# Pool maps and scales multiplied once into the pool projection's weight, and the background work's rates set anew

## The chip, the cores and the metric

The kernel runs on one core of one Trainium2 chip. The metric is the device time of one execution in microseconds, as the median of several runs. TensorE multiplies, VectorE (DVE) and ScalarE (ACT) work element by element, and SyncE (SP) and a few other queues issue transfers between device memory and on-chip memory.

## The reference

One residual block over 2048 tokens of width 1024, all in fp32:

```python
h = rmsnorm(x, norm_mix_pre)
proj = h @ w_in                                   # pool 512 | GLU 1024 | gate_a 1024 | gate_b 1024
pooled = trailing_mean_minus_self(u_pool, ...)    # 4 groups of 128 channels, windows 2, 4, 8, 16
mixed = einsum('bsgc,gcd->bsgd', pooled, pool_w) * pool_scale
branch_a = mixed @ w_pool_out
branch_b = silu(layernorm(causal_depthwise_conv(a * sigmoid(g), 31 taps))) @ w_conv_out
merged = sigmoid(g_a) * branch_a + sigmoid(g_b) * branch_b
x = x + rmsnorm(merged @ w_o)
f = square(relu(rmsnorm(x) @ w_up)) @ w_down
x = x + rmsnorm(f)
```

The part that matters here is branch A: a 128x128 matrix `pool_w[g]` for each group, a scale for each channel, and then the projection `w_pool_out` (512 by 1024). All three are linear, and nothing stands between them.

## The kernel before

The 2048 tokens are worked on as two batches (`b`) of 1024, each with two halves (`t`) of 512. Every fp32 operand of a product is split into a high part and a low part of a shorter format: ScalarE casts the high part (`split`, `split_w`, line L202 or L209), VectorE subtracts it to get the low part (`sub`, L123). Each product of blocks is then three passes of 128x512 matmuls (high by high, low by high, high by low; `matmuls`, L252).

The large projections save products as Strassen's method does: an `Octet` covers a group of blocks with 7 products instead of 8. Its weights are sums and differences of raw weight blocks (`weight_parts`: raw loads `wr`, sums `ws`, high and low parts `wh` and `wl`), its tokens sums and differences of token blocks (`token_parts`: `big`, `tr`). `START` and `ORDER` list the order of the 7 products; `run_octets` goes through them. In batch 0, the first GLU octet is followed by the second (`o2`) interleaved with the pool octet (`pi`, from about 69 to 142 us), and then by the octets of gate a (`ga`) and gate b (`gb`), until about 307 us. Then come branch A of batch 0 (`branch_a`: mixed tokens times `w_po`), the same projections of batch 1 with the second half of the work of batch 0 in the background, both merges with the output projection, and the two large MLP products `up` and `down`, the longest part.

What isn't a product of an octet runs in the background. A generator yields after each small step, and a `Lane(rate, generators)` takes `rate` steps of its generators at every product (`bg()`); `yield n` skips n products. Such work is the convolution's taps (`conv_steps`, one VectorE operation a tap, L918, accumulating in `y`), the pool steps, the statistics of batch 1 (`in_stats`) and the norm of the convolution (`norm_steps`, which reloads the taps' sums `yd` and lets TensorE sum over channels, `rb`). A background instruction is tied to come behind the product at which it was taken. Nearly every load, and many stores, are issued by SP one after the other; some stores by ScalarE. A scheduler orders the instructions of each engine; `tc.high_priority(offset=n)` lets a block of code stand n instructions earlier in its priorities, as far as data allows.

The pool branch: `more()`, called at a given product of `pi`, runs `pool_weight()` (loads `w_pool`, splits it into `pw`) and adds `pool_steps(0)` to the lane `tail`. For each group `pool_steps` sums the window (VectorE), subtracts the token, splits the result (`split`), multiplies it with `pw` (6 matmuls into the accumulator `mix`), scales it while ScalarE copies it out, and stores it to `mxd`. `branch_a` reads it back and multiplies it with `w_po`. The lines that fix the pace:

```python
tail = Lane(1.3, conv_steps(0, (0,)))                  # 3 from more() on
lanes += [Lane(3.2, *rest, marked(norm_steps(0, 1), "norm"))]
lanes.append(Lane(1.7, marked(pool_steps(1, False), "pool")))
```

Of the kernel before, what the change touches and what calls it, by code (L numbers as in the profile page):

```python
# [15 lines left out]
P = 128  # L16
D = 1024
SEQ = 2048
T = 512
# [49 lines left out]
def block_kernel(  # L69
# [58 lines left out]
    def load(o, src):  # L128
        return nc.sync.dma_start(o, src)
# [150 lines left out]
    def weight_parts(src, key, b, keep, raw):  # L280


        s = {}

        def get(q):
            if q not in raw:
                raw[q] = mk(p_wr, "wr")
                load(raw[q], src[q])
            return raw[q]

        def minus(a, b, op=sub):
            o = mk(p_ws, "ws")
            op(o, a, b)
            return o

        def source(i):
            if i in (1, 2, 4):
                return get({1: 0, 2: 1, 4: 3}[i])
            if (key, i, "sum") in kept and b:
                if ("s", i) not in raw:  # L300
                    raw["s", i] = mk(p_wr, "wr")
                    load(raw["s", i], kept[key, i, "sum"])
                return raw["s", i]
            if i == 7:
                return minus(get(0), get(2))
            if i in (5, 6) and 1 not in s:
                s[1] = minus(get(2), get(3), add)
            if i == 6:
                s[2] = minus(s[1], get(0))
                return s[2]  # L310
            if i == 5:
                return s[1]
            return minus(get(1), s[2])

        def save(i, what, tile):
            kept[key, i, what] = dram("kept")
            later.append((kept[key, i, what], f32(tile)))

        def part(i):
            with tc.high_priority(offset=ahead[0]):  # L320
                for q in {1: (0,), 2: (1,), 4: (3,), 7: (0, 2), 5: (2, 3), 6: (2, 3, 0), 3: (1,)}[i]:
                    if (key, i, "sum") not in kept or not b:
                        get(q)
                if (key, i, "sum") in kept and b:
                    source(i)
            with tc.high_priority(offset=60):
                t = source(i)
                w = raw.pop(("w", i), None)
                if w is None and not ((key, i, "low") in kept and b):
                    w = split_w(t)  # L330
            if (key, i, "low") in kept and b:
                with tc.high_priority(offset=80):
                    w = split_w(t, low=kept[key, i, "low"])
            if keep and not b:
                save(i, "low", w[1])
                if keep == "sums" and i not in (1, 2, 4):
                    save(i, "sum", t)
            return w

        return part  # L340
# [652 lines left out]

    pw = [p_const.tile([P, CW], F32R, tag=f"pw{i}", name=f"pw{i}") for i in (0, 1)]

    def pool_weight():
        raw = mk(p_wr, "wr")[:, :CW]
        load(raw, w_pool)
        nc.scalar.copy(pw[0], raw)
        sub(pw[1], raw, f32(pw[0]))  # L1000

    def pool_steps(b, alone):

        def get(g):
            s, u = window(W), tr()
            load(s, ud[g][:, b * TB : b * TB + W])
            load(u, ud[g][:, HALO + b * TB : HALO + b * TB + TB])
            return s, u

        s, u = get(0)  # L1010
        yield 1
        for g in range(CC):
            w, m = WINDOWS[g], 1
            while m < w:
                lo = HALO - (w - 2 * m)
                s2 = window(W) if alone or m in (2, 8) else mk(p_ss, "r", F32, (P, W))
                add(s2[:, lo:], s[:, lo:], s[:, lo - m : W - m])
                s, m = s2, 2 * m
                yield
            if b == 0:  # L1020
                mul(
                    s[:, HALO : HALO + w],
                    s[:, HALO : HALO + w],
                    cst[:, C_CNT + g * HALO : C_CNT + g * HALO + w],
                )
            nc.vector.scalar_tensor_tensor(
                u, s[:, HALO:], 1.0 / w, u, op0=ALU.mult, op1=ALU.subtract
            )
            hl = split(u, *TR)
            if g + 1 < CC:  # L1030
                s, u = get(g + 1)
            yield 3
            ps = psum("mix")
            for t in (0, 1):
                h = slice(t * T, (t + 1) * T)
                matmuls(ps[:, h], pw, g, [tuple(p[:, h] for p in hl)], main=False)
            o = tr()
            nc.scalar.activation(o, ps, AF.Copy, scale=col(C_PSC + g))
            yield
            load(mxd[b, g, 0], o)  # L1040
            yield

    def cell_of(d, homes):

# [31 lines left out]
    def branch_a(b, mixed, bg):  # L1076


        def gate_of(k):
            sg = tr()  # L1080
            load(sg, sad[(b, *k)])
            return sg

        keys = [(c, t) for c in range(CPS) for t in (0, 1)]
        for (c, t), sg in ahead_by_one(keys, gate_of, 2):
            if t == 0:
                w = load_w(w_po[c], ("po", c))
            ps = psum("A")
            for q in (0, 1):
                i = matmuls(ps[:, q * T : (q + 1) * T], w, CC * q, half(mixed, t))  # L1090
            mark(i)
            flush()
            with tc.high_priority(offset=URGENT):
                mark(mul(sg, ps, sg))
            load(mad[b, c, t], sg)
            bg()
# [374 lines left out]
    o2, = glu(0, parts, ahead_raw[:1])  # L1471
    tail = Lane(1.3, conv_steps(0, (0,)))
    stats = Lane(1, in_stats(1))

    def then(f, o, at=4):

# [9 lines left out]

    def more():
        ahead[0] = AHEAD
        pool_weight()
        tail.gens.append(chain_of(pool_steps(0, True), conv_steps(0, (1, 2, 3), False)))  # L1490
        tail.rate = 3

    pi = pool_in(0, parts, ahead_raw[1])[0]
    ahead[0] = 45
    lanes.append(tail)
    then(lambda: lanes.append(stats), o2, 4)
    run(
        [o2],
        [then(more, pi, 4)],
        gate(0, parts, 3, sad, "ga", "lows"),  # L1500
        gate(0, parts, 5, sbd, "gb", "sums"),
    )
    stats.empty()
    rest = tail.gens
    mixed = fetch(mxd, 0)
    parts = Parts(lambda ops: input_parts(1, ops))
# [11 lines left out]
        yield from gen  # L1518

    rest = [marked(chain_of(*rest), "conv")]  # L1520
    lanes += [Lane(3.2, *rest, marked(norm_steps(0, 1), "norm"))]

    def pooling():
        lanes[0].rate = 3.2
        lanes.append(Lane(1.7, marked(pool_steps(1, False), "pool")))
        lanes.append(Lane(2.0, behind_all(conv_steps(1, (0, 1, 2, 3)), "conv", "pool")))


# [7 lines left out]
    )  # L1536
    conv1 = lanes.pop()
    empty()
    conv1.rate = 0.5
    lanes.append(conv1)  # L1540
    merged = merge(0, bg)
    fetched = []
# [16 lines left out]

    parts.need(2)  # L1560
    branch_a(1, mixed, step)
    conv1.rate = 1.2
    conv1.gens.append(norm_steps(1, 3))
    lanes.append(conv1)
    def faster():
        conv1.rate = 2.8

    octs = mlp_up(0, parts)
    then(faster, octs[0])
    run(octs)  # L1570
    empty()
    early.close()
# [469 lines left out]
```

## Time and profile before

| | us |
|---|---|
| median of 3 runs | 2219.32 (2218.80 to 2219.84) |
| profiled execution, its own time | 2218.82 |
| span of that execution, first to last instruction | 2216.9 |
| TensorE busy | 2168.8 (98%) |
| VectorE busy | 1683.1 (76%) |
| ScalarE busy | 1047.7 (47%) |

The mean granted clock of TensorE is 0.991 of full speed. A profile row such as `PE glu L252 <- ACT wh L209: 3.8, 1, 3.8` says that TensorE's matmuls into `glu` of line 252 waited 3.8 us in total, in 1 event, the longest 3.8, for ScalarE's instruction that wrote `wh` in line 209. A timeline row has the start in us, the time to the end of a group of alike instructions, the engine, line and operation, `out<-in`, sizes, how many, and in brackets the idle time before it and what ended it. A matmul's own duration (about 390 ns) overlaps its neighbours'.

### The profile page before, as it was taken

The numbers are of one execution on the slowest core, as the hardware profiler recorded it, in microseconds if no ns is written. First come the engines' busy times: TensorE is split into PE (matmuls) and PEld (weight loads), VectorE is DVE, ScalarE is ACT, GpSimd is POOL, SyncE is SP. The second block draws the span as 40 slices with busy tenths as digits, with TensorE's granted clock in tenths as the row PEclk, the third lists the DMA queues.
The fourth block names the chain that finished last, engine by engine and source line by source line (L and its number), as shares of the span: only waits on it lengthen the run. The fifth ranks groups of instructions, "written<-read, shape, count | busy, mean of one in ns | idle before, by whom it ended". The sixth has DMA issues, their size and how long they took to land.

```text
span 2216.9 us, 25038 instructions
## 1 busy us (share of the span) xinstructions
PE 2168.8 (98%) x9580; PEld 1787.5 (81%) x9580; DVE 1683.1 (76%) x1637; ACT 1047.7 (47%) x1102; POOL 20.6 (1%) x39
## 2 busy tenths in 40 slices
PE   9999999999999999999999999999999999999996
PEld 7777888778788888888888878788878888888875
DVE  8988688996789899977757857876644656696767
ACT  5434453334443535455735766665444222224553
POOL 0000000000000000000000000000000000000001
PEclk9999999999999999999999999999999999999998
DMA  4678898777997788354786778885957545446798
GB/s 169 242 286 300 294 364 291 240 246 273 328 376 258 250 328 293 144 210 153 273 306 234 249 264 287 330 312 210 357 196 233 181 155 189 149 146 224 267 306 253
DMA packets 157863, 563.31 MB, mean 254 GB/s; under 512 B 18576, under 2 KB 18704, under 8 KB 157712
## 3 DMA queue, kind: packets, MB, share of 16 engines
q1 hardware_dynamic: 141040, 500.90, 63.7%
q10 hardware_dynamic: 12672, 46.14, 5.3%
q0 software_dynamic: 4032, 14.68, 2.5%
q8 instruction: 75, 1.23, 0.2%
q14 instruction: 44, 0.36, 0.1%
HBM read 374.39 MB, written 188.31 MB: 254 GB/s over the span
## 4 chain that ended last, share of the span: by engine, by line
PE 82%; DVE 7%; DMA 6%; ACT 2%; issue 2%; SPq 0%; DVEq 0%; ACTq 0%; POOL 0%; POOLq 0%
PE down L252 26%; PE up L252 24%; PE wo L252 7%; PE gb L252 6%; PE glu L252 5%; PE B L252 4%; PE ga L252 4%; PE A L252 3%; DMA wr<-w_in 1%; DVE y L918 1%; DMA fo<-x1d 1%; PE pool L252 1%; DVE wl L123 1%; DVE tr L120 1%; PE rb L458 1%
## 5 line engine op out<-in xcount | busy, mean ns | idle before, releaser
L252 PE MATMUL up<-big,wh 128*128 128x512 f32 x1792 | 482.3, 390 | 1.7 <-DVE big L123 1.5
L252 PEld LDWEIGHTS up<-big,wh 128*128 128x128 f32 x1792 | 337.1, 188 | 73.2 <-DVE big L123 2.7
L209 ACT CAST wh<-wr 128x1024 fp32r<-128x1024 f32 x169 | 177.6, 1051 | 301.9 <-PE up L252 72.9
L252 PE MATMUL down<-tr,wh 128*128 128x512 f32 x800 | 312.5, 391 | 0.0
L918 DVE SCALAR_TENSOR_TENSOR y<-v,cst,y 128x1024 f32<-128x1024 f32 x240 | 307.7, 1282 | 2.8
L252 PE MATMUL down<-fo,wh 128*128 128x512 f32 x784 | 302.6, 391 | 1.1 <-ACT fo L1703 1.1
L252 PE MATMUL up<-big,wl 128*128 128x512 f32 x896 | 276.6, 390 | 0.0
L252 PE MATMUL down<-fo,wl 128*128 128x512 f32 x768 | 238.4, 392 | 2.8 <-DMA wl<-lows 2.8
L209 ACT CAST wh<-ws 128x1024 fp32r<-128x1024 f32 x118 | 123.9, 1051 | 212.4 <-PE up L252 63.3
L120 DVE TENSOR_TENSOR big<-big,down 128x1024 f32<-128x1024 f32 x88 | 107.0, 1219 | 121.5 <-PE down L252 111.7
L252 PEld LDWEIGHTS up<-big,wl 128*128 128x128 f32 x896 | 168.3, 188 | 34.9
L1703 ACT CAST fo<-tr 128x1024 fp32r<-128x1024 f32 x86 | 86.9, 1052 | 206.6 <-PE down L252 133.8
L123 DVE TENSOR_TENSOR wl<-ws,wh 128x1024 fp32r<-128x1024 f32 x110 | 134.3, 1221 | 58.6 <-ACT wh L209 54.4
L252 PEld LDWEIGHTS down<-tr,wh 128*128 128x128 f32 x800 | 150.9, 189 | 31.3
L252 PEld LDWEIGHTS down<-fo,wh 128*128 128x128 f32 x784 | 147.6, 188 | 32.3 <-ACT fo L1703 1.6
L252 PEld LDWEIGHTS down<-fo,wl 128*128 128x128 f32 x768 | 145.2, 189 | 33.4 <-DMA wl<-lows 3.2
L123 DVE TENSOR_TENSOR wl<-wr,wh 128x1024 fp32r<-128x1024 f32 x99 | 120.8, 1220 | 20.3 <-ACT wh L209 19.3
L123 DVE TENSOR_TENSOR tr<-tr,fo 128x1024 fp32r<-128x1024 f32 x86 | 101.8, 1220 | 43.8 <-ACT fo L1703 43.8
L252 PE MATMUL wo<-big,wh 128*128 128x512 f32 x480 | 128.8, 390 | 0.0
L252 PE MATMUL ga<-big,wh 128*128 128x512 f32 x448 | 121.1, 392 | 2.7 <-ACT tr L408 1.8
L252 PE MATMUL glu<-big,wh 128*128 128x512 f32 x432 | 117.9, 394 | 6.0 <-ACT wh L209 3.8
L252 PE MATMUL gb<-big,wh 128*128 128x512 f32 x448 | 120.9, 392 | 0.0
(196 smaller groups left out, 3367.1 us busy)
## 6 DMA issues: line engine op xcount, KB each, us to landing
tr<-fd SPq DMA_DIRECT2D x110, 512.0 KB, 4.5
wl<-kept SPq DMA_DIRECT2D x81, 512.0 KB, 4.5
kept<-wl SPq DMA_DIRECT2D x74, 512.0 KB, 5.5
wr<-w_down SPq DMA_DIRECT2D x68, 512.0 KB, 4.7
wr<-w_up SPq DMA_DIRECT2D x64, 512.0 KB, 4.4
wr<-w_in SPq DMA_DIRECT2D x56, 512.0 KB, 5.2
fd<-tr ACTq DMA_DIRECT2D x54, 512.0 KB, 3.6
fd<-tr SPq DMA_DIRECT2D x48, 512.0 KB, 3.5
```

Of the source, the lines that this page charges most:

```text
L120: return nc.vector.tensor_tensor(o, a, b, op=ALU.add)
L123: return nc.vector.tensor_tensor(o, a, b, op=ALU.subtract)
L209: nc.scalar.copy(hi[:, :n], src[:, :n])
L252: i = nc.tensor.matmul(ps, w[wp][:, (at + k) * P : (at + k + 1) * P], rhs[k][xp], start=start and n == 0, stop=stop and n == len(order) - ...
L458: nc.tensor.matmul(st[:, at + g : at + g + 1], ss[:, g * P : (g + 1) * P], inv_n, start=start is None or (start and g == 0), stop=stop, sk ...
L918: nc.vector.scalar_tensor_tensor(acc, v[:, k : k + TB], wk, acc, op0=ALU.mult, op1=ALU.add)
L1703: nc.scalar.copy(hi, t)
```

## The change

Since the three maps are linear, `pool_w`, `pool_scale` and `w_pool_out` are multiplied together on the chip once. A new generator `pool_weights` runs in a lane of its own (`weights`, rate 2), beside the second GLU octet's end and the first gate: it loads `w_pool` (which the host now hands over transposed), scales its four 128x128 blocks by `pool_scale`, splits them into `pw`, loads each of the four 128-row blocks of `w_pool_out`, splits it, multiplies (6 `mix` matmuls a block), copies the result and stores it in four pieces of 128 KB into `w_pp`, from which `branch_a` loads its weights in both batches. `pool_steps` stores the window differences themselves to `mxd`; its split, its matmuls and its scaling copy are gone. Beside that, the offset of the weight sums in `weight_parts` goes from 60 to 100, `stats` is added after product 5 of `o2` (which comes earlier than product 4), `more` after product 3 of `pi` (one earlier than product 4), and several rates differ.

```diff
@@ -323,7 +323,7 @@
                         get(q)
                 if (key, i, "sum") in kept and b:
                     source(i)
-            with tc.high_priority(offset=60):
+            with tc.high_priority(offset=100):
                 t = source(i)
                 w = raw.pop(("w", i), None)
                 if w is None and not ((key, i, "low") in kept and b):
@@ -993,11 +993,39 @@
 
     pw = [p_const.tile([P, CW], F32R, tag=f"pw{i}", name=f"pw{i}") for i in (0, 1)]
 
-    def pool_weight():
-        raw = mk(p_wr, "wr")[:, :CW]
-        load(raw, w_pool)
-        nc.scalar.copy(pw[0], raw)
-        sub(pw[1], raw, f32(pw[0]))
+    w_pp = [dram("wpp", (P, D)) for _ in range(CPS)]
+
+    def pool_weights():
+
+        yield 2
+        raw = tr()
+        load(raw[:, :CW], w_pool)
+        for g in range(CC):
+            part = raw[:, g * P : (g + 1) * P]
+            nc.scalar.activation(part, part, AF.Copy, scale=col(C_PSC + g))
+        nc.scalar.copy(pw[0], raw[:, :CW])
+        sub(pw[1], raw[:, :CW], f32(pw[0]))
+        yield
+
+        def get(g):
+            t = tr()
+            load(t, w_po[g])
+            return t
+
+        for g, t in ahead_by_one(range(CC), get):
+            hi, lo = split(t, *TR)
+            yield 3
+            ps = psum("mix")
+            for h in (0, 1):
+                n = slice(h * T, (h + 1) * T)
+                matmuls(ps[:, n], pw, g, [(hi[:, n], lo[:, n])], main=False)
+            w = tr()
+            nc.scalar.copy(w, ps)
+            yield
+            for c in range(CPS):
+                load(w_pp[c].rearrange("p (q k m) -> p q k m", q=2, k=CC)[:, :, g],
+                     w[:, 2 * c * P : 2 * (c + 1) * P].rearrange("p (q m) -> p q m", q=2))
+            yield
 
     def pool_steps(b, alone):
 
@@ -1026,19 +1054,13 @@
             nc.vector.scalar_tensor_tensor(
                 u, s[:, HALO:], 1.0 / w, u, op0=ALU.mult, op1=ALU.subtract
             )
-            hl = split(u, *TR)
             if g + 1 < CC:
-                s, u = get(g + 1)
-            yield 3
-            ps = psum("mix")
-            for t in (0, 1):
-                h = slice(t * T, (t + 1) * T)
-                matmuls(ps[:, h], pw, g, [tuple(p[:, h] for p in hl)], main=False)
-            o = tr()
-            nc.scalar.activation(o, ps, AF.Copy, scale=col(C_PSC + g))
+                s, n = get(g + 1)
             yield
-            load(mxd[b, g, 0], o)
-            yield
+            load(mxd[b, g, 0], u)
+            if g + 1 < CC:
+                u = n
+            yield 1
 
     def cell_of(d, homes):
 
@@ -1084,7 +1106,7 @@
         keys = [(c, t) for c in range(CPS) for t in (0, 1)]
         for (c, t), sg in ahead_by_one(keys, gate_of, 2):
             if t == 0:
-                w = load_w(w_po[c], ("po", c))
+                w = load_w(w_pp[c], ("po", c))
             ps = psum("A")
             for q in (0, 1):
                 i = matmuls(ps[:, q * T : (q + 1) * T], w, CC * q, half(mixed, t))
@@ -1471,6 +1493,7 @@
     o2, = glu(0, parts, ahead_raw[:1])
     tail = Lane(1.3, conv_steps(0, (0,)))
     stats = Lane(1, in_stats(1))
+    weights = Lane(2, pool_weights())
 
     def then(f, o, at=4):
 
@@ -1486,21 +1509,22 @@
 
     def more():
         ahead[0] = AHEAD
-        pool_weight()
+        lanes.append(weights)
         tail.gens.append(chain_of(pool_steps(0, True), conv_steps(0, (1, 2, 3), False)))
         tail.rate = 3
 
     pi = pool_in(0, parts, ahead_raw[1])[0]
     ahead[0] = 45
     lanes.append(tail)
-    then(lambda: lanes.append(stats), o2, 4)
+    then(lambda: lanes.append(stats), o2, 5)
     run(
         [o2],
-        [then(more, pi, 4)],
+        [then(more, pi, 3)],
         gate(0, parts, 3, sad, "ga", "lows"),
         gate(0, parts, 5, sbd, "gb", "sums"),
     )
     stats.empty()
+    weights.empty()
     rest = tail.gens
     mixed = fetch(mxd, 0)
     parts = Parts(lambda ops: input_parts(1, ops))
@@ -1518,11 +1542,11 @@
         yield from gen
 
     rest = [marked(chain_of(*rest), "conv")]
-    lanes += [Lane(3.2, *rest, marked(norm_steps(0, 1), "norm"))]
+    lanes += [Lane(2.4, *rest, marked(norm_steps(0, 1), "norm"))]
 
     def pooling():
-        lanes[0].rate = 3.2
-        lanes.append(Lane(1.7, marked(pool_steps(1, False), "pool")))
+        lanes[0].rate = 2.8
+        lanes.append(Lane(1.4, marked(pool_steps(1, False), "pool")))
         lanes.append(Lane(2.0, behind_all(conv_steps(1, (0, 1, 2, 3)), "conv", "pool")))
 
 
@@ -1536,7 +1560,7 @@
     )
     conv1 = lanes.pop()
     empty()
-    conv1.rate = 0.5
+    conv1.rate = 0
     lanes.append(conv1)
     merged = merge(0, bg)
     fetched = []
@@ -1559,14 +1583,14 @@
 
     parts.need(2)
     branch_a(1, mixed, step)
-    conv1.rate = 1.2
-    conv1.gens.append(norm_steps(1, 3))
+    conv1.rate = 0.9
+    conv1.gens.append(norm_steps(1, 2))
     lanes.append(conv1)
     def faster():
-        conv1.rate = 2.8
+        conv1.rate = 3.4
 
     octs = mlp_up(0, parts)
-    then(faster, octs[0])
+    then(faster, octs[1])
     run(octs)
     empty()
     early.close()
@@ -2022,8 +2046,8 @@
         "xt": g["x"].reshape(NB, 2, T, CPS, 2, P).transpose(0, 3, 1, 5, 4, 2).reshape(NB, CPS, 2, P, TB),
         "xm": g["x"].reshape(NB, 2, G, P, D),
         "w_in": octets(g["w_in"], IN_OCTS),
-        "w_pool": g["pool_w"].transpose(1, 0, 2).reshape(P, CW),
-        "w_po": pairs(g["w_pool_out"]).reshape(4, P, D),
+        "w_pool": g["pool_w"].transpose(2, 0, 1).reshape(P, CW),
+        "w_po": g["w_pool_out"].reshape(4, P, D),
         "w_co": pairs(g["w_conv_out"]).reshape(4, P, D),
         "w_o": octets(g["w_o"], ((0, 2), (1, 3))),
         "w_up": octets(g["w_up"], up_octs),
```

How the order of instructions moves, at three places. The first is VectorE at the second GLU octet and the pool octet, of batch 0. `wl<-wr,wh` is the split of a raw weight, `ws<-wr,wr` a sum of raw weights, `big` and `tr` are token parts, `y` is a convolution tap, `tr<-glu,tr` an add on a finished product. Before:

```order
L123 TENSOR_TENSOR tr_682<-big_227,big_213 128x1024
L123 TENSOR_TENSOR tr_703<-big_229,tr_674 128x1024
L123 TENSOR_TENSOR tr_711<-big_231,tr_682 128x1024
L123 TENSOR_TENSOR big_685<-tr_682,big_684 128x1024
L120 TENSOR_TENSOR tr_782<-glu_756,tr_747 128x1024
L123 TENSOR_TENSOR big_706<-tr_703,big_705 128x1024
L123 TENSOR_TENSOR big_714<-tr_711,big_713 128x1024
L123 TENSOR_TENSOR wl_822<-wr_382,wh_821 128x1024
```

and a little later

```order
L123 TENSOR_TENSOR tr_923<-big_231,big_227 128x1024
L123 TENSOR_TENSOR big_920<-tr_917,big_919 128x1024
L123 TENSOR_TENSOR wl_999<-ws_996,wh_998 128x1024
L123 TENSOR_TENSOR big_926<-tr_923,big_925 128x1024
L918 SCALAR_TENSOR_TENSOR y_785<-v_749,cst,y_785 128x1024
L120 TENSOR_TENSOR ws_1055<-wr_1049,wr_1051 128x1024
L120 TENSOR_TENSOR tr_992<-glu_879,tr_955 128x1024
L123 TENSOR_TENSOR ws_1057<-ws_1055,wr_1053 128x1024
```

After, at the same two places:

```order
L123 TENSOR_TENSOR tr_686<-big_231,big_217 128x1024
L123 TENSOR_TENSOR wl_826<-wr_386,wh_825 128x1024
L123 TENSOR_TENSOR tr_707<-big_233,tr_678 128x1024
L123 TENSOR_TENSOR big_689<-tr_686,big_688 128x1024
L123 TENSOR_TENSOR tr_715<-big_235,tr_686 128x1024
L120 TENSOR_TENSOR tr_786<-glu_760,tr_751 128x1024
L123 TENSOR_TENSOR big_710<-tr_707,big_709 128x1024
L914 TENSOR_SCALAR y_789<-v_753,cst 128x1024
L123 TENSOR_TENSOR big_718<-tr_715,big_717 128x1024
```

```order
L123 TENSOR_TENSOR big_924<-tr_921,big_923 128x1024
L123 TENSOR_TENSOR tr_927<-big_235,big_231 128x1024
L120 TENSOR_TENSOR tr_1000<-glu_883,tr_959 128x1024
L120 TENSOR_TENSOR ws_1069<-wr_1063,wr_1065 128x1024
L123 TENSOR_TENSOR big_930<-tr_927,big_929 128x1024
L123 TENSOR_TENSOR ws_1071<-ws_1069,wr_1067 128x1024
L918 SCALAR_TENSOR_TENSOR y_789<-v_753,cst,y_789 128x1024
```

The last of the four raw-weight splits (`wl_822` before, `wl_826` after) moves from the end of the first piece to its beginning, six rows earlier; in the second piece `big_926` stood ahead of the add and the sum `ws_1055`, and its counterpart `big_930` stands behind both.

The second place is ScalarE at the first gate octet; `CAST wh` makes the high part of a weight, `COPY tr<-ga` empties an accumulator of the gate. Before:

```order
L209 CAST wh_1483<-ws_1481 128x1024
L209 CAST wh_1522<-ws_1520 128x1024
L209 CAST wh_1570<-wr_1404 128x1024
L408 COPY tr_1440<-ga_1305 128x1024
L408 COPY tr_1476<-ga_1450 128x1024
```

After, where `pw`, `tr_1414` and `tr_1426` belong to the new lane:

```order
L209 CAST wh_1575<-ws_1573 128x1024
L1005 ACTIVATE tr_1414<-tr_1414,cst 128x128 x4
L1006 CAST pw_206<-tr_1414 128x512
L202 CAST tr_1426<-tr_1422 128x1024
L408 COPY tr_1468<-ga_1333 128x1024
L655 ACTIVATE tr_1412,st_1368<-tr_1412 128x1024
L209 CAST wh_1649<-wr_1432 128x1024
L408 COPY tr_1507<-ga_1481 128x1024
```

The copy of the first accumulator (`tr_1440` before, `tr_1468` after) stood behind the cast `wh_1570`, and now stands ahead of its counterpart `wh_1649`, with the new lane's scalings and casts before it.

The third place is SP at the reload of the taps' sums for the norm of batch 0 (`tr<-yd`), among the weight loads of the second gate of batch 1 (`w_in`) and of the merge (`w_co`). Before:

```order
L129 DMA tr_4592<-yd_162 128x1024
L129 DMA wl_4734<-kept_2332 128x1024
L129 DMA tr_4633<-yd_163 128x1024
L129 DMA wr_4874<-w_in 128x1024
L129 DMA zd_169<-tr_4554 128x1024
L129 DMA wl_4770<-kept_2369 128x1024
L129 DMA wr_4937<-w_co 128x1024
L129 DMA tr_4676<-yd_164 128x1024
```

After:

```order
L129 DMA tr_4342<-yd_162 128x1024
L129 DMA v_4391<-vd_90 128x1054
L129 DMA wl_4482<-kept_2103 128x1024
L129 DMA wr_4622<-w_in 128x1024
L129 DMA tr_4381<-yd_163 128x1024
L129 DMA zd_169<-tr_4304 128x1024
L129 DMA wr_4657<-w_in 128x1024
L129 DMA wl_4518<-kept_2152 128x1024
L129 DMA tr_4426<-yd_164 128x1024
L129 DMA wr_4694<-w_in 128x1024
```

Before, the last reload (`tr_4676`) stood behind a load of `w_in` and one of `w_co`; now its counterpart (`tr_4426`) comes while loads of `w_in` are still to be issued, and ahead of all of `w_co`. The SP rows also show `v<-vd`, the taps' input of the next batch, ahead of the last two reloads.

## The prediction

> **What bounds the kernel now.** I read the page's busy times and its chain first, then who made TensorE wait.
>
> ```profile
> PE 2168.8 (98%) x9580; PEld 1787.5 (81%) x9580; DVE 1683.1 (76%) x1637; ACT 1047.7 (47%) x1102; POOL 20.6 (1%) x39
> PE 82%; DVE 7%; DMA 6%; ACT 2%; issue 2%; SPq 0%; DVEq 0%; ACTq 0%; POOL 0%; POOLq 0%
> ```
>
> TensorE is busy 2168.8 of 2216.9 us, so only two things can shorten the kernel much: fewer matmuls, or fewer stalls in the 48 us that are left. The waits of TensorE by what released them:
>
> ```profile
> PE glu L252 <- ACT wh L209: 3.8, 1, 3.8
> PE rb L458 <- DVE sm L120: 2.9, 1, 2.9
> PE ga L252 <- ACT tr L408: 1.8, 1, 1.8
> PE glu L252 <- DVE tr L120: 1.8, 1, 1.8
> PE pool L252 <- DVE tr L120: 1.5, 1, 1.5
> PE pool L252 <- DVE wl L123: 1.5, 1, 1.5
> PE ga L252 <- DVE wl L123: 0.9, 2, 0.5
> ```
>
> Each is one or two events; the first three, the last and the second-last lie where the change moves work. Windows by stage (columns: time, PE, PEld, DVE, ACT, POOL busy, granted clock, DMA share, GB/s):
>
> ```profile
> 69.00:142.00 73.00, 67.66 (x291) 55.19 (x290) 68.69 (x61) 33.09 (x35) 0.00 (x0) 0.98 0.76 261
> 142.00:227.00 85.00, 81.41 (x348) 65.88 (x347) 70.78 (x85) 38.72 (x45) 0.00 (x0) 0.98 0.82 307
> 227.00:307.00 80.00, 80.00 (x354) 66.25 (x353) 55.06 (x50) 38.04 (x40) 0.00 (x0) 1.00 0.86 308
> 307.00:350.00 43.00, 43.00 (x191) 35.42 (x191) 41.42 (x36) 20.79 (x26) 0.00 (x0) 1.00 1.00 380
> 350.00:637.00 287.00, 279.94 (x1231) 230.31 (x1230) 238.38 (x216) 127.35 (x128) 0.00 (x0) 0.99 0.80 281
> ```
>
> In 69 to 142 us (second GLU octet and pool octet) VectorE is full and TensorE loses 5.3 us; in 142 to 307 us (gates of batch 0) VectorE has 85.00 - 70.78 + 80.00 - 55.06 = 39.2 us free and TensorE loses 3.6; in 307 to 350 us the DMA engines are full and TensorE loses nothing.
>
> **The change, part by part.**
>
> *Matmuls.* 48 `mix` matmuls (4 groups, 2 batches, 6 each) become 24, once, on the weight.
>
> ```profile
> 226.49 1.36 PE mix L252 x6
> 545.91 1.37 PE mix L252 x6
> ```
>
> In the chain six of them take 1.36 us, so one costs 0.227 us of the path (its own record, about 390 ns, overlaps its neighbours'). 24 x 0.2267 = -5.4 us. No other work hides them, since TensorE runs without a gap around them. The weight's extra work (four 128x128 scalings, four casts and subtractions) replaces eight casts and subtractions of the tokens, so ScalarE and VectorE get less, not more: 0.
>
> *The octet of 69 to 142 us* (offset 60 to 100, stats and weights earlier). The stalls there now:
>
> ```profile
> 77.55 0.98 PE L252 MATMUL pool<-big,wl 128*128 128x512 f32 x3 [1.50 <-DVE wl L123]
> 85.81 2.93 PE L252 MATMUL glu<-big,wh 128*128 128x512 f32 x6 [3.84 <-ACT wh L209]
> 88.54 1.17 PE L252 MATMUL glu<-big,wl 128*128 128x512 f32 x3
> 89.55 0.62 PE L252 MATMUL glu<-big,wh 128*128 128x512 f32 x2
> ```
>
> After the 3.84 us wait six matmuls stand 88.54 - 85.81 = 2.73 us (to the next row's start) instead of 1.36, the next three 1.01 instead of 3 x 0.227 = 0.68: 1.7 us more at half pace. The place costs 1.50 + 3.84 + 1.7 = 7.0 us. Why it waits:
>
> ```profile
> 76.27 1.23 DVE L123 TENSOR_TENSOR wl<-wr,wh 128x1024 fp32r<-128x1024 f32 x1
> 83.45 1.22 DVE L120 TENSOR_TENSOR ws<-wr,wr 128x1024 f32<-128x1024 f32 x1 [1.76 <-issue]
> 69.64 0.36 SPq L129 DMA_DIRECT2D wr<-w_in  x1
> 77.56 0.33 SPq L129 DMA_DIRECT2D wr<-w_in  x1
> ```
>
> The split at 76.27 stands behind token parts; it gives TensorE its low half late, and frees the buffer into which SP loads the next raw weight (77.56), whose sum `ws` comes at 83.45. In the order after, this split stands six rows earlier and SP issues both loads back to back, so both stalls lose their cause. But the same VectorE work is due before the octet's end, and what is pushed back are token parts: `big_930`, due five or six matmuls (1.1 to 1.4 us) after the product that ends at matmul 359, now stands behind `tr_1000`, an add that waits for that product, and behind `ws_1069`. Three operations of 1.22 us (add, `ws`, `big`) against 1.4 us of cover: a stall of at least 3 x 1.22 - 1.4 = 2.3 us, and more if VectorE arrives late. Ends: nothing is late next, -7.0; VectorE's lateness is all kept and the add's chain comes on top, +3.5 (2.3 + 1.2 for one late operation). I take the stall as moved and slightly dearer, +1.3, since VectorE is 68.69 of 73.00 us busy and loses no instruction there.
>
> The Trainium skill (TensorE: Matmul & The Clock Gate, What's actually happening) says that the clock halves only after an idle window of about 3.4 us, which runs freely. By it the 3.84 us wait costs the slow stretch and waits under 3.4 us mostly do not, so two stalls of 2 us would be cheaper than one of 4: the sum would fall by about 1.7 us. The row of 167.16 below has the slow stretch after 1.82 us, and I go by the rows.
>
> *First gate, 142 to 170 us.*
>
> ```profile
> 167.16 2.48 PE L252 MATMUL ga<-big,wh 128*128 128x512 f32 x6 [1.82 <-ACT tr L408]
> 169.44 1.48 PE L252 MATMUL ga<-big,wl 128*128 128x512 f32 x3
> 170.72 0.82 PE L252 MATMUL ga<-big,wh 128*128 128x512 f32 x2
> 171.38 0.40 PE L252 MATMUL ga<-big,wl 128*128 128x512 f32 x1
> 165.15 1.04 ACT L209 CAST wh<-wr 128x1024 fp32r<-128x1024 f32 x1
> 166.10 1.92 ACT L408 COPY tr<-ga 128x1024 f32<-128x1024 f32 x2
> ```
>
> The copy that frees the accumulator stands behind the cast of 165.15, which waits for a weight buffer. In the order after, the copy comes ahead of that cast and has only the cast of the `w_po` load before it. That saves 1.82 and the slow stretch behind it: (169.44 - 167.16) - 1.36 = 0.92, (170.72 - 169.44) - 0.68 = 0.60, (171.38 - 170.72) - 0.45 = 0.21, together 1.7. The two waits `ga <- DVE wl` (0.9 together in the list of waits) are on splits that stand earlier too. Together -4.4; ends -4.4 and 0 (the load of `w_po` is late and holds the copy as long).
>
> *The norm of batch 0, 560 to 578 us* (rates lower, taps done sooner).
>
> ```profile
> 559.44 0.49 SPq L129 DMA_DIRECT2D tr<-yd  x1
> 565.13 1.23 DVE L123 TENSOR_TENSOR tr<-tr,r 128x1024 f32<-128x1024 f32 x1 [7.92 <-DMA tr<-yd]
> 572.37 2.21 PE L458 MATMUL rb<-inv_c,sm 128*128 128x1 f32 x16 [2.88 <-DVE sm L120]
> 574.44 2.05 PE L252 MATMUL gb<-big,wh 128*128 128x512 f32 x4
> 576.30 1.33 PE L252 MATMUL gb<-big,wl 128*128 128x512 f32 x3
> 577.47 0.63 PE L252 MATMUL gb<-big,wh 128*128 128x512 f32 x2
> 1013.50 1.84 PE L458 MATMUL rb<-inv_c,sm 128*128 128x1 f32 x16
> 1015.20 1.16 PE L252 MATMUL up<-big,wh 128*128 128x512 f32 x4
> ```
>
> The statistics matmuls wait for the last reload of the taps' sums. Cost: 2.88, and (577.47 - 572.37) minus 1.70 + 0.91 + 0.68 at full pace (sixteen small ones, four, three) = 1.8: together 4.7 us. By the order, this reload may go out 51 main matmuls ahead of them now and 72 in the changed kernel; 21 x 0.227 = 4.8 us more room, above 2.88. So -4.7; ends -4.7 and 0.
>
> *New waits.* A new order of taps, splits and loads makes new collisions that I cannot place. Nearest rows: single waits of VectorE's adds, 1.5 and 1.8 us, each with or without 1.7 of slow pace. I take one of each and one slow stretch, 1.5 + 1.8 + 1.7 = +5.0; ends 0 and +10 (three with slow pace: 3 x (1.65 + 1.7)).
>
> *Traffic.* Added: four 512 KB loads and sixteen 128 KB stores of 512-byte pieces, 4096 pieces.
>
> ```profile
> q1 hardware_dynamic: 141040, 500.90, 63.7%
> ```
>
> A packet of that queue takes 0.637 x 16 x 2216.9 / 141040 = 0.160 us at 3.55 KB; a piece takes between 0.023 (by bytes) and 0.160 us, hence 6 to 41 us of all 16 engines, beside 26.5 us free in 142 to 307 us (0.18 x 85 + 0.14 x 80). Where DMA stands at 1.00 (307 to 350) TensorE does not wait, so I take 0; ends 0 and +8 (14.5 us over, about half of which reaches a weight).
>
> The Trainium skill (DMA: Bandwidth & Descriptors, Specifications) gives 512 B as the smallest transfer at line rate. By that these pieces would be at the cheap end, about 6 us, and this term stays 0.
>
> *The taps' rates.*
>
> ```profile
> L918 DVE SCALAR_TENSOR_TENSOR y<-v,cst,y 128x1024 f32<-128x1024 f32 x240 | 307.7, 1282 | 2.8
> ```
>
> By the order, 25 more `y` taps fall before branch A of batch 0: 25 x 1.28 = 32 us of VectorE, hidden by the 39.2 us counted above; if that cover were gone, each us short would be a us of TensorE.
>
> Sum: -5.4 + 1.3 - 4.4 - 4.7 + 5.0 + 0 = -8.2 us. The profiled execution took 2218.8 us, 0.5 below the median of the runs, so 2219.3 - 8.2 = 2211 us.
>
> **Rivals.**
> *Only the matmuls go.* The stalls at the gate and the norm turn up elsewhere at the same price. For it: VectorE is 94% busy in 69 to 142 us, and what is late there moves on. Against it: two of the three have a cause that the order removes. -5.4 + 1.3 = -4.1, and any further wait of 1.5 us takes it to about -2.5: 2216 us.
>
> *VectorE runs full in the gates (slower).* Place: 142 to 307 us. Only 7 us of its 39.2 stay free after the taps. In 69 to 142 us it could not use 4.3 of 73 us, 6%; 6% of 165 us is 10, so it would be 3 us short, with two slow stretches 3 + 3.4 = +6.4, which nearly eats the gain: 2217. If it cannot use 24 us (350 to 637 us shows 17% idle, at lower demand), it is 17 short: -8.2 + 17 + 3.4 = +12, 2231 us. It decides from about 16 us unusable. Against it: taps are background work that can slip without TensorE noticing, if they stand behind what it needs.
>
> *The pieces are dear (slower).* At 0.160 us each, weights of the second gate arrive late: -8.2 + 8 + 5 for the waits that follow with slow pace = +5, 2224 us. SP, which issues 20 more transfers at 0.33 to 0.49 us (8 us, in order), would hold the weight loads queued behind them. Against it: 1.00 of DMA without a wait of TensorE.
>
> *The stall of the octet goes altogether.* If `big_930` is not late, -7.0 in place of +1.3, and 2203 us.
>
> **How the numbers follow.** Forecast 0.48; octet's stall gone 0.18; only the matmuls 0.20; VectorE full 0.08; dear pieces 0.06. A measurement tells about 0.2%, 4.4 us, from no change. Faster by more than that: all of the forecast and the octet's case and a little of the third, 0.68; within: most of the third and a little of the slower ones, 0.19; slower 0.13. The range from 2201 to 2223 us leaves out the ends where everything fits (-5.4 - 7.0 - 4.4 - 4.7 = -21.5, 2198) and the two dear cases' upper parts.
>
> **What would show it.** `mix` x24 in the chain at 1.36 us per six; no wait near 78 and a new one of 2 to 5 us on `big` or `wh` near 98 us; no `ga <- ACT tr` wait near 166; no `rb <- DVE sm` wait near 570; VectorE at 95% or more in 142 to 307 us; the sixteen stores with a few us to landing. I am wrong if VectorE delays gate weights there (several `ga` or `gb` waits on `wl` or `tr`), or if TensorE waits there for `wl` or `wr` by DMA.

## The result, and the profile after

| | before | changed |
|---|---|---|
| median of 6 runs, us | 2219.33 (2215.73 to 2225.07) | 2212.21 (2208.23 to 2215.49) |
| ratio of the runs | | 0.9965, 95% interval 0.9949 to 0.9981 |
| profiled execution, its own time | 2218.82 | 2215.49 |

The changed kernel is 0.35% faster, 7 us, where 2211 us was forecast. Its profiled execution is the slowest of its six, so the two profiles differ by 3.3 us only. Three executions with the same instructions up to some 430 us (the changed kernel and the two kernels named e7 and e8 below) begin branch A of batch 0 at 306.7, 309.5 and 306.2 us: one landmark of one execution is good to about 3 us.

The busy line of the page, and the waits of TensorE by what released them (us in total, times, longest), of the changed kernel:

```profile
PE 2165.7 (98%) x9556; PEld 1784.4 (81%) x9556; DVE 1677.5 (76%) x1633; ACT 1040.2 (47%) x1098; POOL 20.6 (1%) x39
...
PE glu L252 <- DMA wl<-kept: 4.0, 1, 4.0
...
PE gb L252 <- DVE tr L120: 2.4, 2, 2.0
...
PE glu L252 <- DVE big L123: 1.8, 1, 1.8
PE rb L458 <- DVE sm L120: 1.7, 1, 1.7
...
PE glu L252 <- ACT big L202: 1.2, 1, 1.2
```

The waits on `wh`, `wl` and `ga <- ACT tr` of before are gone; new are those of `glu` on `big`, of the second gate (`gb`) on `tr`, and a dearer one on a reloaded weight (`wl<-kept`: 0.9 us before, 4.0 now). The windows of before, read again (time, PE, PEld, DVE, ACT, POOL busy, granted clock, DMA share, GB/s):

```profile
69.00:142.00 73.00, 68.93 (x287) 55.08 (x286) 71.40 (x74) 34.79 (x38) 0.00 (x0) 0.95 0.83 297
142.00:227.00 85.00, 84.99 (x375) 70.00 (x374) 77.48 (x83) 41.29 (x49) 0.00 (x0) 1.00 0.91 331
227.00:307.00 80.00, 77.56 (x334) 63.37 (x333) 76.07 (x66) 35.19 (x36) 0.00 (x0) 0.98 0.89 319
307.00:350.00 43.00, 43.00 (x191) 35.61 (x190) 40.01 (x36) 19.87 (x26) 0.00 (x0) 1.00 0.95 361
```

In 142 to 227 us TensorE no longer stops. In 227 to 307 us VectorE goes from 55.06 to 76.07 us busy (31 taps instead of 8), and TensorE, which did not wait there, now loses 2.4 us and some of its clock.

Where each stage begins, read off the first matmul of the stage in TensorE's timeline, in us (`ga`, `gb`: gates of batch 0; A, B: branches of batch 0 and of the merge; norm: the statistics of the convolution's norm of batch 0):

| kernel | pool octet | ga | gb | A | norm | B | first up | span |
|---|---|---|---|---|---|---|---|---|
| before | 69.1 | 141.9 | 227.7 | 307.1 | 572.4 | 636.5 | 816.7 | 2216.9 |
| changed | 69.3 | 143.0 | 224.5 | 306.7 | 528.6 | 631.9 | 814.3 | 2213.7 |
| e1, fold only | 69.0 | 149.1 | 243.5 | 321.5 | 537.2 | 650.5 | 837.9 | 2238.7 |
| e2, all but the fold | 68.9 | 142.2 | 222.1 | 300.9 | 585.0 | 632.8 | 836.6 | 2246.1 |
| e3, offset 60 | 70.8 | 148.1 | 237.5 | 315.3 | 530.4 | 631.9 | 813.8 | 2215.7 |
| e5, offset and triggers | 69.6 | 142.7 | 222.5 | 301.4 | 560.2 | 633.2 | 818.5 | 2214.2 |
| e6, fold, old rates | 70.9 | 143.3 | 224.9 | 307.7 | 517.6 | 634.7 | 823.4 | 2230.1 |
| e9, offset alone | 69.3 | 144.2 | 227.6 | 306.9 | 570.3 | 634.6 | 817.6 | 2222.6 |
| e10, triggers alone | 69.0 | 144.3 | 224.2 | 303.0 | 556.3 | 630.1 | 812.4 | 2212.9 |
| e11, fold, old triggers | 69.0 | 142.7 | 239.2 | 317.5 | 550.4 | 646.5 | 827.5 | 2223.4 |
| e12, fold, old rates, yields | 69.0 | 141.6 | 223.2 | 302.1 | 564.6 | 626.9 | 817.6 | 2215.7 |

(The span's 0 is the first instruction. From the first up product to the end, the changed kernel, e4 and e7, which have the same instructions there, take 1399.4, 1396.1 and 1397.0 us: differences of some 3 us there are chance.)

### The profile page after: what moved, and what is told of

It is laid out like the page before. It is cut to its first block, busy times and chain, and to the rows that moved or that the text cites. A ratio compares the mean times of both kernels' runs of the same rounds, so it can differ in the third digit from the quotient of the medians.

```text
span 2213.7 us, 25020 instructions
## 1 busy us (share of the span) xinstructions
PE 2165.7 (98%) x9556; PEld 1784.4 (81%) x9556; DVE 1677.5 (76%) x1633; ACT 1040.2 (47%) x1098; POOL 20.6 (1%) x39
## 4 chain that ended last, share of the span: by engine, by line
PE 76%; DVE 9%; DMA 9%; issue 2%; ACT 2%; SPq 0%; DVEq 0%; ACTq 0%; POOL 0%; POOLq 0%
PE down L252 26%; PE up L252 22%; PE glu L252 6%; PE wo L252 6%; PE B L252 4%; PE A L252 4%; PE ga L252 3%; PE gb L252 3%; PE pool L252 2%; DVE y L918 2%; DVE wl L123 1%; DMA tr<-yd 1%; DVE tr L120 1%; DMA fo<-x1d 1%; DMA kept<-ws 1%
```

## The experiments

Every kernel was timed against the kernel before on the same chip. That chip was another for e1 to e4, e5 to e8 and e9 to e12, and the changed kernel was timed apart from all of them, so kernels are compared by their ratios; the difference of two ratios is good to about 0.2%, 5 us. "Fold" is the product of the maps, the scales and `w_pool_out`; "rates" are the lanes' rates and the two late edits that go with them (`norm_steps` and the place of `faster`).

### Which part brings the gain: e1, e2

e1 has the fold alone. e2 has everything else:

```diff
 # e1: the changed kernel with
-            with tc.high_priority(offset=100):
+            with tc.high_priority(offset=60):
-    then(lambda: lanes.append(stats), o2, 5)
+    then(lambda: lanes.append(stats), o2, 4)
-        [then(more, pi, 3)],
+        [then(more, pi, 4)],
 # and the rates of before
 # e2: the kernel before with offset 100, products 5 and 3, and the new rates
```

> Only the folding of the maps into the projection's weight; offset, triggers and rates as before. Theory A (the 24 matmuls are the gain, 5.4 us on the path): 5 us faster than before, and the stalls of before near 78, 86, 167 and 572 us still there. Rival B (the new rates and offset are the gain, the fold alone collides with the gate's weights): within 2 us of before, with new ga or gb waits of several us.

> Everything but the fold: offset 100, new triggers, new rates, with the 48 mix matmuls of before. Theory A: 1 to 3 us faster than before (waits of the first gate and the norm gone, new ones in the octet and the second gate). Rival B: 6 to 7 us faster, all of the change's gain.

Measured: e1 1.0093 (1.0078 to 1.0108), 20 us slower than before; e2 1.0100 (1.0086 to 1.0115), 22 us slower. Both theories (A, the matmuls; B, the rates and the offset) fall. Each half of the change is a loss of some 20 us, and together they are a gain of 7: the parts don't add.

Why e2 is slow is read where branch B begins: from there to the first up product it takes 203.8 us, the kernel before 180.2, which is about all of its 22. Timelines of e2, TensorE and then SP's issues:

```profile
632.81 0.79 PE L252 MATMUL B<-big,wh 128*128 128x512 f32 x1 [5.40 <-ACT big L1050]
636.55 1.93 PE L252 MATMUL B<-big,wh 128*128 128x512 f32 x3 [2.95 <-DVE big L123]
640.65 0.79 PE L252 MATMUL B<-big,wh 128*128 128x512 f32 x1 [2.17 <-ACT big L1050]
646.95 0.79 PE L252 MATMUL B<-big,wh 128*128 128x512 f32 x1 [2.97 <-ACT big L1050]
```

```profile
634.27 0.45 SPq L129 DMA_DIRECT2D zd<-tr  x1
...
640.79 0.32 SPq L129 DMA_DIRECT2D big<-zd  x1
```

The fourth channel block of the convolution's result is stored (`zd<-tr`) at 634.27 us and reloaded at 640.79, while TensorE could begin at 627 (632.81 less its wait). Before, the last store was issued at 620.12 us and in the changed kernel at 578.05. So the lower rates alone bring taps and norm too late; with the old rates (e5 below) no wait of TensorE at the start of branch B is over 0.6 us. With the fold they don't: the pool steps then no longer skip three products a group, and the taps behind them in the same lane come sooner (31 of them in 227 to 307 us of the changed kernel, 11 in e2).

### What keeps the fold's lane harmless: e11

The changed kernel with the two old triggers:

```diff
-    then(lambda: lanes.append(stats), o2, 5)
+    then(lambda: lanes.append(stats), o2, 4)
-        [then(more, pi, 3)],
+        [then(more, pi, 4)],
```

> The changed kernel with the two old triggers (fold, offset and new rates kept). Theory H (the new lane's w_pool must land before the first gate's accumulator is copied, which the earlier trigger gives): a wait of 5 us on the copy near 184 us, behind a ScalarE wait on w_pool, and 8 us or more slower at 307 us. Rival (the offset alone is enough for that): no such wait, within 3 us of the changed kernel.

Measured: 1.0023 (1.0011 to 1.0035), 0.58% or 13 us slower than the changed kernel. Theory H holds: the wait is there, and branch A begins 10.8 us later. Timelines of e11, TensorE, ScalarE and SP:

```profile
177.46 2.08 PE L252 MATMUL ga<-big,wh 128*128 128x512 f32 x4 [5.33 <-ACT tr L408]
```

```profile
173.62 1.28 ACT L1005 ACTIVATE tr<-tr,cst 128x128 f32<-128x128 f32 x4 [7.28 <-DMA tr<-w_pool]
174.93 0.62 ACT L1006 CAST pw<-tr 128x512 fp32r<-128x512 f32 x1
175.45 1.04 ACT L202 CAST tr<-tr 128x1024 fp32r<-128x1024 f32 x1
176.40 1.00 ACT L408 COPY tr<-ga 128x1024 f32<-128x1024 f32 x1
```

```profile
162.30 0.33 SPq L129 DMA_DIRECT2D kept<-wl  x1
167.42 0.33 SPq L129 DMA_DIRECT2D wr<-w_in  x1
167.80 0.42 SPq L129 DMA_DIRECT2D kept<-wl  x1
168.28 0.42 SPq L129 DMA_DIRECT2D tr<-w_pool  x1
```

The load of `w_pool` stands on SP behind a weight load that goes out only at 167.42; ScalarE waits 7.28 us for it, and the copy that frees the gate's accumulator stands behind. One product earlier this is gone; of the changed kernel:

```profile
161.51 1.28 ACT L1005 ACTIVATE tr<-tr,cst 128x128 f32<-128x128 f32 x4 [0.68 <-DMA tr<-w_pool]
162.83 0.62 ACT L1006 CAST pw<-tr 128x512 fp32r<-128x512 f32 x1
163.41 1.06 ACT L202 CAST tr<-tr 128x1024 fp32r<-128x1024 f32 x1
164.37 1.00 ACT L408 COPY tr<-ga 128x1024 f32<-128x1024 f32 x1
```

The same four rows, 0.68 us of wait, and no wait of TensorE. e1 has the bad form too (5.16 us at 183.76).

### Offset and triggers: e3, e5, e9, e10

e3 is the changed kernel with the offset back at 60. e5 is the kernel before with the offset and the triggers but neither fold nor new rates; e9 and e10 have only the one or the other:

```diff
 # e3: the changed kernel with
-            with tc.high_priority(offset=100):
+            with tc.high_priority(offset=60):
 # e9: the kernel before with
+            with tc.high_priority(offset=100):
 # e10: the kernel before with
+    then(lambda: lanes.append(stats), o2, 5)
+        [then(more, pi, 3)],
 # e5: both
```

> The changed kernel with the offset of the weight sums back at 60. Theory (the stall of the octet is moved, not removed): waits of about 1.5 and 3.8 us come back at 78 and 86 us in place of those of 1.2 and 1.8 us at 100 and 103 us, the stretch 69 to 142 us stays within 1.5 us, and the time within 2 us of the changed kernel. Rival (the earlier sums are worth the stall): 4 to 7 us slower than the changed kernel.

> The kernel before with the new offset and the two new triggers, without the fold and with the lanes' rates of before. Theory C (the lower rates alone make the run without the fold slow, since taps and norm come too late for branch B and the MLP): within 4 us of before, no wait of B on the reload of zd at 633 us and none of up near 1025 and 1060 us. Rival (the offset or the triggers do it): 15 us or more slower than before, like the rates-only kernel.

> The kernel before with the offset of the weight sums at 100 and nothing else. Theory F (the offset moves the octet's stall and clears the gate's, which is all of the gain of the no-fold kernel): 8 to 12 us faster than before. Rival G (the earlier triggers do it, since with the offset back at 60 the changed kernel lost little): within 3 us of before.

> The kernel before with statistics and pool work started earlier (products 5 and 3) and nothing else. Theory G: 6 to 12 us faster than before. Theory F: within 3 us of before.

Measured: e3 0.9970 (0.9958 to 0.9982); e9 0.9972 (0.9958 to 0.9986); e10 0.9962 (0.9947 to 0.9978); e5 0.9947 (0.9930 to 0.9964). The offset and the triggers, on a kernel that keeps its 48 `mix` matmuls and its rates, bring 12 us, and each of them alone about 6 to 8, each of these to 3 or 4. No kernel of this study has a lower ratio than e5, and its interval overlaps that of the changed kernel: fold and new rates together bring nothing that can be measured on top of it (0.9965 against 0.9947). Theory C (the rates make e2 slow) holds in that e5 is not slow, though it forecast no gain of 12 us. Theory F (the offset is all of the gain) and theory G (the offset does nothing, the triggers do it) both fall, since each part has a gain of its own.

In which stage e5's 12 us arise is not shown. In its profile branch B begins 3.3 us earlier than before and the first up product 1.8 us later; from there to the end it takes 1395.7 us against 1400.2, hardly more than the chance differences above.

e3 is 1 us slower than the changed kernel, to about 4, so its theory fits and only the upper part of its rival (4 to 7 us) falls. In its profile the waits of before come back as foretold (1.48 us at 79, 3.79 us at 87), but 69 to 142 us grows by 3.6 us, more than the 1.5 that was allowed, and branch A begins 8.6 us later than in the changed kernel; the first gate alone is 7.9 us longer, with a wait of 4.42 us for VectorE at 205 us. By branch B nothing of it is left: 631.91 us against 631.90. The changed kernel, which has the lead, gives it back in waits (4.02 us for `wl<-kept` at 367 us, 1.67 us for the norm at 529 us) that e3 doesn't have.

Which of the two clears the first gate is seen in e9, the timeline of TensorE with the offset alone:

```profile
167.98 1.65 PE L252 MATMUL ga<-big,wh 128*128 128x512 f32 x6 [1.82 <-ACT tr L408]
169.47 0.84 PE L252 MATMUL ga<-big,wl 128*128 128x512 f32 x3
```

The wait of before stands there unchanged; in e10 it is gone. So the triggers clear the gate, and the offset the octet's first two stalls. Only the first shortens its stage: from `ga` to `gb` e10 takes 79.8 us instead of 85.8. From the pool octet to `ga` e9 takes 74.9 us and e10 75.3, before 72.8; e9 waits 3.11 and 1.53 us at the place to which the stall moved.

### Fold with the old rates: e6, e12

e6 is e5 with the fold. e12 also lets `pool_steps` skip three products a group, as it did when it waited for its split:

```diff
 # e6: the changed kernel with the rates of before;  e12: e6 with
+            yield 3
             yield
             load(mxd[b, g, 0], u)
```

> The changed kernel with the lanes' rates of before (fold, offset and triggers kept). Theory C (the fold alone was slow because its lane started one product later with the lower offset, so w_pool landed late ahead of an accumulator's copy): within 5 us of the changed kernel. Rival D (the old rates overfill VectorE once the pool lane is short): 10 us or more slower than the changed kernel, with new waits of TensorE on VectorE after 350 us.

> Fold, offset and triggers with the old rates, and the pool steps skip three products a group again where they used to wait for the split. Theory D (the fold with the old rates is slow because the shorter pool lane lets the taps crowd VectorE): the waits near 262, 302 and 397 us go and it is 10 us or more faster than fold with old rates, near or under the no-fold kernel. Rival (the new lane's loads, splits and stores are what costs): within 4 us of fold with old rates.

Measured: e6 1.0022 (1.0005 to 1.0038), 17 us slower than e5 and 13 us slower than the changed kernel, as rival D has it; e12 1.0002 (0.9988 to 1.0017). With e2 this makes all four combinations on the new offset and triggers: neither fold nor new rates (e5) 0.9947, the fold alone (e6) 1.0022, the rates alone (e2) 1.0100, both (the changed kernel) 0.9965. Each alone is a loss, of 17 and 34 us, and together they cost 4 us, to about 5.

A part of e6's loss is seen in its second gate. Timelines of e6, VectorE and TensorE:

```profile
256.75 1.22 DVE L123 TENSOR_TENSOR wl<-wr,wh 128x1024 fp32r<-128x1024 f32 x1
257.88 2.60 DVE L918 SCALAR_TENSOR_TENSOR y<-v,cst,y 128x1024 f32<-128x1024 f32 x2
260.40 1.22 DVE L120 TENSOR_TENSOR tr<-gb,tr 128x1024 f32<-128x1024 f32 x1
```

```profile
261.67 1.65 PE L252 MATMUL gb<-big,wh 128*128 128x512 f32 x6 [2.27 <-DVE tr L120]
```

Taps (`y`) stand ahead of the add that TensorE waits for; at 302 us it waits another 1.80 us for one. With the yields VectorE is free again; windows of the second gate in e6 and in e12:

```profile
227.00:307.00 80.00, 75.93 (x331) 61.47 (x330) 75.88 (x65) 35.01 (x36) 0.00 (x0) 1.00 0.89 321
```

```profile
227.00:307.00 80.00, 78.96 (x349) 65.08 (x348) 50.45 (x46) 36.11 (x38) 0.00 (x0) 1.00 0.91 321
```

VectorE falls from 75.88 to 50.45 us busy, branch A begins at 302.1 instead of 307.7 us (1.8 us of this were there when `ga` began) and B at 626.9, earliest of all kernels. Of the waits that theory D names, the one near 262 us is gone and the one near 302 us down to 1.04 us. The third, e6's wait of 1.88 us for `big` near 397 us, stays: e12 waits 1.87 us for it at 388 us, and e5, without the fold, 2.73.

D's 10 us in the time are not there: e12 is 0.20%, 4.4 us, faster than e6, with overlapping intervals, and still 12 us slower than e5. That is about what the rival allowed (within 4 us: the new lane's own loads, splits and stores are what costs). Up to branch A nothing of such a cost is seen, for e12 begins it at 302.1 us and e5 at 301.4; later e12 gives its lead back at the start of branch B (2.6 us) and beside branch A of batch 1, where TensorE waits 3.8 us for `tr`. So the crowding by taps is shown as one cause, and what makes up most of the 17 us stays open. The yields in batch 0 alone weren't tried.

### The price of 24 matmuls: e4, e7, e8

The changed kernel with 24 matmuls more: e4 repeats the weight's, e7 puts idle ones where batch 1 had its own, e8 into the first up product.

```diff
 # e4
-            for h in (0, 1):
+            for h in (0, 1, 0, 1):
 # e7, in pool_steps, for batch 1 (e8: the same in a lane beside the up product)
+                ps = psum("mix")
+                for t in (0, 1):
+                    h = slice(t * T, (t + 1) * T)
+                    matmuls(ps[:, h], pw, g, [(pw[0], pw[1])], main=False)
```

> The changed kernel with each of the weight's 24 mix matmuls done twice, so 48 as before. Theory A (a matmul of 0.227 us is wholly on the path): 5.4 us slower than the changed kernel, six rows of 2.7 us for one group in the chain. Rival (TensorE's extra time is absorbed where it would wait for VectorE next): 1 to 3 us slower.

> The changed kernel with 24 idle matmuls (6 per group, on the maps themselves, their result unused) where the pool steps of batch 1 had theirs, with no split or copy. Theory E (in batch 1 too the extra TensorE time is taken up by waits that end at a time set by transfers): 0 to 2 us slower than the changed kernel. Theory A (these are the 24 that the change saved, wholly on the path): 5.4 us slower.

> The changed kernel with the same 24 idle matmuls in the first up product (817 to 1125 us), where TensorE did not wait. Theory E: 5.4 us slower than the changed kernel, for nothing there absorbs them; the stretch of the up product longer by 5.4 us. Rival (they only take up slack there too): under 2 us.

Measured: 0.9969 (0.9954 to 0.9985), 0.9962 (0.9947 to 0.9976), 0.9968 (0.9953 to 0.9984), against 0.9965 of the changed kernel: +0.9, -0.7 and +0.7 us, each to about 5 us. In the profiles the matmuls do take their time. The first up product, windows of e8 and of e7, which has none there:

```profile
812.48:1126.70 314.22, 314.16 (x1393) 259.94 (x1392) 237.73 (x217) 173.85 (x174) 0.53 (x1) 1.00 0.58 210
```

```profile
820.87:1129.17 308.30, 308.30 (x1370) 255.59 (x1368) 236.76 (x216) 173.78 (x174) 0.53 (x1) 1.00 0.58 214
```

314.22 - 308.30 = 5.9 us where 5.4 were expected. In e8's profile they are still there at the end (1405.3 us from the first up product, against 1396.1 to 1399.4 in the changed kernel, e4 and e7), though not in its median: theory E's 5.4 us for e8 show in the stretch and not in the time. In e7 the stretch from the last start of `glu` in batch 1 (415 us) to branch B takes 222.5 us, against 217.3 to 220.3 in the changed kernel, e3, e4 and e8: 2 to 5 us. In e4, branch A begins 4 us later than the mean of the three executions without the extra (307.5) and B 0.5 us later than in the changed kernel: waits may have taken up the rest, but single landmarks are good to 3 us only. So a matmul is 0.227 us where TensorE doesn't wait afterwards; that it is less where it does fits e4 and is not shown. What remains of 24 of them in the whole time is less than the runs resolve.

## Why the prediction was right, and where not

**The total** was right: -8.2 us forecast, -7.1 measured. Its parts were not all right.

**Matmuls, -5.4.** The size is what e8 shows for a stretch without waits. It is not what made the kernel faster: e5 keeps all 48 and is about as fast or faster. The step that is not borne out is that no other work hides them: with its new rates, the fold that saves them is worth nothing that the runs resolve on top of offset and triggers, and 24 of them put back cost -0.7 to +0.9 us, to about 5. None of the rivals had a gain without the matmuls.

**The octet, +1.3.** Measured 73.68 us against 72.83, +0.85. The stall moved to the place that was named. The changed kernel, VectorE and TensorE:

```profile
99.15 1.22 DVE L120 TENSOR_TENSOR tr<-glu,tr 128x1024 f32<-128x1024 f32 x1
100.28 1.21 DVE L120 TENSOR_TENSOR ws<-wr,wr 128x1024 f32<-128x1024 f32 x1
101.41 1.22 DVE L123 TENSOR_TENSOR big<-tr,big 128x1024 fp32r<-128x1024 f32 x1
```

```profile
100.36 0.50 PE L252 MATMUL glu<-big,wh 128*128 128x512 f32 x1 [1.24 <-ACT big L202]
102.68 0.79 PE L252 MATMUL glu<-big,wh 128*128 128x512 f32 x1 [1.83 <-DVE big L123]
103.27 1.48 PE L252 MATMUL glu<-big,wl 128*128 128x512 f32 x3
```

Add, sum of weights, `big`: 1.24 + 1.83 = 3.1 us of wait and a slow stretch behind it, where 2.3 or more was worked out from the order.

**First gate, -4.4.** From `ga` to `gb` 85.77 us became 81.51, with one more group of `mix` (1.36): -5.6. The size was right, with the later wait on `tr` (0.9 us) gone as well. That the copy would come in time hangs on the trigger's one product: e11 is the case that the prediction kept as the other end, with a price above that end (5.3 us).

**The norm, -4.7: mis-sized.** It waits 1.67 us now and runs slow for about 1.7 more, so about 1.3 us were gained (4.7 lost before, 3.4 now). The reload has its room in the order, but the matmuls come 44 us earlier too. This is one execution: in e3, e4, e7 and e8, with the same fold and rates, these matmuls do not wait at all, which is the full -4.7 of the forecast.

**New waits, +5.0: too small.** The second gate costs 4.2 us (82.2 against 79.4 us with a group of `mix` less), the wait for `wl<-kept` with its slow stretch 4.7: 8.9 us. The cause of the first is that of the rival "VectorE runs full": 76.07 of 80 us busy in the second gate, with two waits of `gb` on `tr`, the sign by which the prediction said it would be wrong. It came true in part, at 4.2 us where its bad case was priced at 20.4. The second wait was released by a transfer, and what made that late was not followed. Against these stands a wait at 464 us of before, 1.9 us on `tr` with the pace behind it, which went without being counted. With 5.4 for the matmuls, which is not measured here, the terms -5.4 + 0.85 - 5.6 - 1.3 + 8.9 - 1.9 come to -4.5 us, and branch B begins 4.6 us earlier. The other 2.5 us of the 7.1 are not in this pair of profiles, whose later stages differ by some 3 us from one execution to the next: no step accounts for them, and the closeness of the total is partly luck.

**Traffic, 0.** Right as far as seen: the sixteen stores of 512-byte pieces fall into 142 to 307 us, where the DMA share is 0.91 and 0.89, and the waits there are on VectorE. The last of them are issued from 250.16 us on, over 100 us ahead of the wait for `wl<-kept`.

## What to carry to other kernels

Where background work is spread by rates, an edit that shortens a background step changes the pace of everything behind it: time the edit and the pace as a pair, since here, on the same offset and triggers, the edit alone cost 17 us, the pace alone 34, and both together 4, to about 5. Before crediting a saving, put it back as idle work at the same place, and try the small moves of a change without its large one: here moving two starts earlier and one priority were worth as much as the whole. When a lead of 5 to 9 us at one stage is zero two stages later, as between e3 and the changed kernel, list the waits in between; here a wait of 4.02 us for a reload was the largest.

## What the runs showed of the hardware

Whether a wait is followed by TensorE's slow pace can't be read from the wait's length. Before, the wait of 1.82 us at 167.16 is followed by six matmuls in 2.28 us, so at 0.38 us each, and the granted clock is 0.68 in 167 to 169 us and 0.50 in 169 to 171. In e9 the same wait, also 1.82 us, is followed at full pace (169.47 - 167.98 = 1.49 us for six, 0.25 each) with a granted clock of 1.00; so it is in e1 (at 172.87 us) and e11 (at 166.39 us). The Trainium skill (TensorE: Matmul & The Clock Gate, What's actually happening) lets the clock fall after at least one idle window of about 3.4 us, and calls the window free-running. By that no gap of 1.82 us would be enough; here one of four was, and the measurement decides.
